# Products of constants ahead of the data, wider modulation products between the tiles, and silu rows by a broadcast load, in one layer of a diffusion backbone

## The chip, the cores and the metric

The kernel runs on one core of a Trainium2 chip. A core has five engines with queues of their own: TensorE (PE, matrix products; its weight loads are shown as PEld), VectorE (DVE), ScalarE (ACT), GpSimd (POOL) and SyncE (SP, which here only issues DMAs). They meet at semaphores. Operands lie in SBUF, products are summed in PSUM, the rest is in device memory and comes by 16 DMA engines. The metric is the device time of one execution in microseconds, lower is better.

## The reference

One layer works on 256 latent tokens and 256 context tokens of 1024 channels: a gated feed-forward layer with half a residual (both streams), a mixer of a gated delta rule and a state-space scan, and a second feed-forward layer (latent only). The change touches only what stands ahead of the first one:

```python
m  = split(silu(c)     @ w_ada + b_ada, 9)      # latent modulation, 9 x 1024
mc = split(silu(c_ctx) @ w_ada + b_ada, 9)      # context modulation
def ffn_sublayer(x, g, shift, scale, gate, w_gu, w_down):
    h = rmsnorm(x, g) * (1.0 + scale) + shift
    gt, up = split(h @ w_gu, 2)
    return x + 0.5 * gate * ((silu(gt) * up) @ w_down)
x  = ffn_sublayer(x,   norm_g[0], m[0],  m[1],  m[2],  ffn_w_gu[0], ffn_w_down[0])
xc = ffn_sublayer(ctx, norm_g[0], mc[0], mc[1], mc[2], ffn_w_gu[0], ffn_w_down[0])
```

## The kernel before

Activations are held transposed: 8 tiles (k = 0 to 7) of 128 channels on the partitions, with 512 columns, 256 of the latent stream and 256 of the context. A matrix product of full precision is made of three products of rounded operands (`mm3`, lines 213 to 215): high weight by high h, high weight by low h, low weight by high h. A weight tile is loaded (`unit`, line 192, tile `raw`), ScalarE writes its high part `whi` (198), VectorE its low part `wlo` (202). Four `raw`, three `whi` and three `wlo` buffers take turns, for the weights of all stages and for the background modulation columns alike.

`setup` (228) loads the two rows of c (`crow`), a packed constant tile (`spk`) and the four halves of x (`xl`, `xc`). silu(c) is needed twice: as columns (`cTs`, for TensorE) and as rows repeated on all 128 partitions (`cs`, for VectorE). The repeated rows are made by four products of a row of ones with the row of c (253) and four silu activations (254).

`rstd_rows` (343) squares x (ScalarE or GpSimd, by `SQS`), adds the squares, sums them over partitions by products with ones into `pss` (378), takes the reciprocal root (`rsqrt`, VectorE and then GpSimd, 337 and 341) and spreads it over the partitions by products with the identity into `psr` (383); `norm_h` copies that to `rrow` (421).

`ada_first` (274) makes scale and shift of the first norm, tile by tile. For each k there are two blocks (c = 0 shift, c = 1 scale) of a 128 x 1024 weight tile `wada`. A block named in `ADA_PE` is done on TensorE: eight products (301), each with a 128 x 128 piece as weights and two columns of `cTs` streaming, into `pada`. The other blocks are two reductions on VectorE (`ada_col`, 270), one a stream, against `cs`. Before, c = 1 is on TensorE for every k and c = 0 for k < 4. Lines 306, 310 and 311 add the bias and form scale and shift; then `norm_h` makes `ht` (430), its high part `hH` (ScalarE, 432) and its low part `hL` (435).

`ffn` (474) begins with six accumulators (three pairs of 128 output channels), for which the weights of tile k (`wgs`) come as one unit: for each k it takes h and issues 6 x 3 products of 512 columns. The remaining output tiles follow with k as the inner loop. `ada_rest` (317) is a background generator: 56 tiles `wadat` for the other modulation columns, reduced on VectorE while the feed-forward layer runs.

The kernel is written with a tile framework that sets the order of each engine's list before the run, from a priority (`cur_priority`, lower first; `wprio` for weight units), from what is ready, and from the free slots of each buffer tag. Each engine then runs its list strictly in that order. Modulation of tile k has a priority of 100000 * (k - 1) + 100 above the base, the products of tile k - 1 that of 100000 * (k - 1) + 1000: so modulation of tile k + 1 stands ahead of the products of tile k. `pada` takes turns in the PSUM tags `ch` and `sd`; `sd` has one slot, which `pss` and `psr` use too.

Of the kernel before, what the change touches and what calls it, by code (L numbers as in the profile page):

```python
# [72 lines left out]
WSP = ()  # L73
SQS = ("aaaa", "gaga")
KLO = ("dve", "dve")
# [8 lines left out]

ADA_PE = [(k, c) for k in range(8) for c in range(2) if c or k < 4]

# [51 lines left out]
class Kernel:  # L138
# [89 lines left out]
    def setup(self):  # L228
        nc, I = self.nc, self.I
        cr = [self.t4([1, D], "crow") for _ in range(2)]  # L230
        for i in range(2):
            nc.scalar.dma_start(cr[i], I["crow"][:, i])
        spk = self.const([P, 112], "spk")
# [8 lines left out]
        ones = self.ones = self.const([P, P], "ones")  # L242
        nc.vector.memset(ones, 1.0)
        self.mhalf = self.const([P, 1], "mhalf")
        nc.vector.memset(self.mhalf, -0.5)

        self.cTs = self.const([P, KD, 2], "cTs")
        nc.scalar.activation(self.cTs, cT, AF.Silu)
        self.cs = [self.kt([P, D], "cs") for _ in range(2)]
        for i in range(2):  # L250
            for j in range(2):
                pc = self.mm4(2 * i + j)
                nc.tensor.matmul(pc, ones[0:1], cr[i][:, 512 * j:512 * j + 512], start=True, stop=True)
                nc.scalar.activation(self.cs[i][:, 512 * j:512 * j + 512], pc, AF.Silu)
        self.junk = self.t4([P, D], "junk")
# [18 lines left out]
    def ada_first(self):  # L274
# [8 lines left out]
        def load():  # L283
            k = len(loads)
            if k < KD:
                loads.append([self.tp.tile([P, 2, 512], F32, tag="ring", bufs=3, name="wada").rearrange("p a b -> p (a b)")
                              if t == "ring" else getattr(self, t)([P, D], "wada") for t in WAT[k]])
                keep, self.tc.cur_priority = self.tc.cur_priority, base + 100000 * k
                for c in range(2):
                    nc.sync.dma_start(loads[k][c], self.I["wada01"][k, c])  # L290
                self.tc.cur_priority = keep
        for k in range(LDA):
            load()
        for k in range(KD):
            w = loads[k]
            self.tc.cur_priority = base + 100000 * (k - 1) + 100
            pa = self.smp([P, 2, 2], "pada", ("ch", "sd")[k % 2])
            for c in range(2):
                if (k, c) in ADA_PE:
                    for q in range(KD):  # L300
                        nc.tensor.matmul(pa[:, c], w[c][:, q * P:q * P + P], self.cTs[:, q], start=q == 0, stop=q == KD - 1)  # L301
            for c in range(2):
                a = ad[:, k, c]
                b = self.b_ada[:, 8 * c + k:8 * c + k + 1].to_broadcast([P, 2])
                if (k, c) in ADA_PE:
                    V.tensor_tensor(a, pa[:, c], b, op=ALU.add)
                    continue
# [5 lines left out]
            load()  # L313
            self.tc.cur_priority = base + 100000 * k + 1000
            yield sc[:, k], ad[:, k, 0]

# [26 lines left out]
    def rstd_rows(self, streams, name, tag="sd"):  # L343
# [6 lines left out]
        for i, s in enumerate(streams):  # L350
            a = self.t2([P, 2, NL], "sqa")
            b = self.t2([P, 2, NL], "sqb")
            if nt == 4:
                for j in range(4):
# [4 lines left out]
                    else:  # L359
                        nc.gpsimd.tensor_tensor(q, xj, xj, op=ALU.mult)  # L360
                    if j:
# [20 lines left out]
        for t in range(nt):  # L382
            nc.tensor.matmul(pr[:, t * P:t * P + P], r[:, t:t + 1].to_broadcast([P, P]), self.ident, start=True, stop=True)
        return pr

# [88 lines left out]
    def ffn(self, i, hg_, n, bg):  # L474
# [8 lines left out]
        if nf:  # L483
# [4 lines left out]
            if i == 0:  # L488
                for hH, hL, k, cols in hg_:
                    wh, wl = self.unit(I["wgs0"][k], "dve")  # L490
                    for j, a in enumerate(first):
                        sl = slice(j * P, j * P + P)
                        self.mm3(a, wh[:, sl], wl[:, sl], hH[k], hL[k], k == 0, k == KD - 1)
            else:
                hg_ = self.norm_h(2, NL)
# [1132 lines left out]
```

## Time and profile before

| | us |
|---|---|
| three runs | 1342.9, 1339.09, 5015.55 |
| median of them | 1342.9 |
| the profiled execution | 1346.67 |
| its span, first to last instruction | 1345.0 |
| its mean granted TensorE clock | 0.97 |

A profile shows one execution. For each engine it gives the time in which an instruction was under way and the idle time with what ended it; a table of windows gives these for stretches of the span, and the chain of waits follows the work that ended last back to its start. A TensorE row can overlap the next one: the ends of products are modelled, and the distance of their starts is the better measure. In the list of products an f32 product counts as two instructions.

Where the first stage (the six accumulators) lies in the profiled execution: first modulation product at 11.07 us, first product of the stage at 29.83, its last tile from 81.14 on, and the stage's end at 85.3.

### The profile page before, as it was taken

To read this page: it belongs to the slowest core of one execution; us is meant where nothing else is said; L and a number is where in the kernel's file an instruction comes from. 1 tells how busy PE (TensorE), PEld (TensorE's weight loads), DVE (VectorE), ACT (ScalarE), POOL (GpSimd) and SP (SyncE) were. 2 spreads that over 40 slices of the span, in tenths; PEclk is the share of its full clock that TensorE was granted. 3 is DMA by queue.
4 is the path that set the end of the run, shared out by engine and by line. 5 is a ranking of instruction groups with operands and counts; after the bars stand their busy time and mean duration, and the time that the engine had idled before them with its cause. 6 is when DMAs were issued, how large, how long until landed. Compare 5 with 4: busy or idle time off the path is not lost.

```text
span 1345.0 us, 21303 instructions
## 1 busy us (share of the span) xinstructions
PE 1290.2 (96%) x8224; PEld 1108.4 (82%) x8224; DVE 955.1 (71%) x1666; ACT 501.3 (37%) x935; POOL 155.1 (12%) x123
## 2 busy tenths in 40 slices
PE   8999999999999987999899999998899899999997
PEld 6878888888889876889888888854468899999997
DVE  4599387646667976888677788988774466866565
ACT  3222222212236652445423465422223345634433
POOL 1000000000010131000123111333411001000000
PEclk9899999999999988999898999998899899999998
DMA  9256357736632389656542255453446555555552
GB/s 363 92 179 221 118 188 242 233 109 235 214 106 102 110 178 242 193 184 192 153 128 80 93 174 164 150 183 125 162 144 226 174 191 190 192 189 185 179 185 79
DMA packets 133018, 230.27 MB, mean 171 GB/s; under 512 B 46706, under 2 KB 78898, under 8 KB 132788
## 3 DMA queue, kind: packets, MB, share of 16 engines
q1 hardware_dynamic: 106240, 211.43, 49.2%
q10 hardware_dynamic: 26676, 17.47, 4.2%
q8 instruction: 65, 1.06, 0.3%
q14 instruction: 37, 0.30, 0.1%
HBM read 207.79 MB, written 21.07 MB: 170 GB/s over the span
## 4 chain that ended last, share of the span: by engine, by line
PE 64%; issue 15%; DVE 13%; DMA 5%; ACT 1%; POOL 1%; SPq 1%; DVEq 0%; POOLq 0%; ACTq 0%
PE acc L213 16%; PE acc L214 16%; PE acc L215 16%; PE acc L611 3%; PE pada L301 2%; DVE Es L1437 2%; DVE cv L630 2%; DVE Es L1426 1%; PE pn L1227 1%; PE pP L1218 1%; PE pS L1253 1%; DMA Es<-asd 1%; PE pTx L1139 1%; PE ptm L980 1%; DVE Es L1439 1%
## 5 line engine op out<-in xcount | busy, mean ns | idle before, releaser
L198 ACT CAST whi<-raw 128x1024 fp32r<-128x1024 f32 (+1 forms) x208 | 214.4, 1033 | 448.9 <-PE acc L214 397.7
L213 PE MATMUL acc<-hH,whi 128*128 128x512 f32 (+1 forms) x976 | 346.5, 357 | 3.6 <-ACT hH L432 1.8
L214 PE MATMUL acc<-hL,whi 128*128 128x512 f32 (+1 forms) x976 | 345.7, 354 | 0.0
L215 PE MATMUL acc<-hH,wlo 128*128 128x512 f32 (+1 forms) x976 | 344.8, 354 | 0.0
L202 DVE TENSOR_TENSOR wlo<-raw,whi 128x1024 fp32r<-128x1024 f32 (+1 forms) x208 | 251.3, 1210 | 96.1 <-ACT whi L198 94.3
L213 PEld LDWEIGHTS acc<-hH,whi 128*128 128x128 f32 x976 | 186.5, 191 | 27.8 <-ACT hH L432 2.2
L215 PEld LDWEIGHTS acc<-hH,wlo 128*128 128x128 f32 x976 | 186.6, 191 | 23.9
L214 PEld LDWEIGHTS acc<-hL,whi 128*128 128x128 f32 x976 | 186.6, 191 | 22.9
L270 DVE CUSTOM_DVE_ANT_0 junk<-wadat,cs 128x1024 f32<-128x1024 f32 x80 | 97.8, 1222 | 42.4 <-DMA wadat<-in_wadaT 41.7
L214 PE MATMUL acc<-aL,whi 128*128 128x256 f32 (+1 forms) x384 | 122.9, 323 | 0.0
L215 PE MATMUL acc<-aH,wlo 128*128 128x256 f32 (+1 forms) x384 | 122.3, 323 | 0.0
L213 PE MATMUL acc<-aH,whi 128*128 128x256 f32 (+1 forms) x384 | 122.2, 323 | 0.0
L630 DVE SCALAR_TENSOR_TENSOR cv<-cbuf,cc,cv 128x512 f32<-128x512 f32 (+1 forms) x144 | 107.3, 752 | 4.6 <-ACT cv L628 2.6
L611 PE MATMUL acc<-hF,raw 128*128 128x256 f32 x416 | 97.7, 391 | 8.4 <-ACT gth L1071 7.8
L611 PEld LDWEIGHTS acc<-hF,raw 128*128 128x128 f32 x416 | 80.8, 197 | 22.7 <-ACT gth L1071 9.1
L214 PEld LDWEIGHTS acc<-aL,whi 128*128 128x128 f32 x384 | 73.0, 190 | 5.6
L215 PEld LDWEIGHTS acc<-aH,wlo 128*128 128x128 f32 x384 | 72.7, 190 | 5.7
L213 PEld LDWEIGHTS acc<-aH,whi 128*128 128x128 f32 x384 | 72.6, 190 | 5.6
L567 DVE SCALAR_TENSOR_TENSOR xl<-acc,hg,xl 128x256 f32<-128x256 f32 x64 | 30.3, 482 | 47.0 <-PE acc L215 46.5
L1049 PE MATMUL acc<-raw,hF 128*128 128x512 f32 x128 | 59.4, 606 | 0.6 <-DVE zbt L1053 0.6
L372 POOL TENSOR_TENSOR sqa<-sqa,sqb 128x256 f32<-128x256 f32 x12 | 11.5, 962 | 410.6 <-ACT sqb L370 407.7
L1049 PEld LDWEIGHTS acc<-raw,hF 128*128 128x128 f32 x128 | 24.6, 194 | 30.5 <-issue 28.4
(398 smaller groups left out, 2084.0 us busy)
## 6 DMA issues: line engine op xcount, KB each, us to landing
raw<-in_wgu SPq DMA_DIRECT2D x76, 512.0 KB, 3.5
wadat<-in_wadaT SPq DMA_DIRECT2D x56, 512.0 KB, 4.2
raw<-in_wdn SPq DMA_DIRECT2D x44, 512.0 KB, 3.4
wada<-in_wada SPq DMA_DIRECT2D x16, 512.0 KB, 8.9
raw<-in_wg SPq DMA_DIRECT2D x16, 512.0 KB, 3.7
raw<-in_wxs SPq DMA_DIRECT2D x16, 512.0 KB, 3.7
Es<-asd SPq DMA_DIRECT2D x16, 512.0 KB, 4.6
raw<-in_wzB SPq DMA_DIRECT2D x16, 512.0 KB, 3.9
```

The costliest lines, as they stand in the source:

```text
L198: nc.scalar.copy(hi, raw)
L202: engs[i % len(engs)].tensor_tensor(lo[:, c:c + w], raw[:, c:c + w], hi[:, c:c + w].bitcast(F32), op=ALU.subtract)
L213: mm(acc, wh, xh, start=start, stop=False)
L214: mm(acc, wh, xl, start=False, stop=False)
L215: mm(acc, wl, xh, start=False, stop=stop)
L270: self.nc.vector.tensor_tensor_reduce(out=self.junk, in0=w, in1=self.cs[s], scale=1.0, scalar=0.0, op0=ALU.mult, op1=ALU.add, accum_out=out)
L301: nc.tensor.matmul(pa[:, c], w[c][:, q * P:q * P + P], self.cTs[:, q], start=q == 0, stop=q == KD - 1)
L567: nc.vector.scalar_tensor_tensor(out=xs, in0=acc[:, NL * s - g0:NL * s - g0 + NL], scalar=hg[s][:, m:m + 1], in1=xs, op0=ALU.mult, op1=ALU ...
L611: self.nc.tensor.matmul(acc, w[:, k * P:k * P + P], self.hF[:, k], start=k == 0, stop=k == KD - 1)
L630: nc.vector.scalar_tensor_tensor(out=u3, in0=buf[:, 0:R, j:j + 64], scalar=cw[:, j:j + 1], in1=u3, op0=ALU.mult, op1=ALU.add)
L1049: nc.tensor.matmul(accs[t], self.hF[:, k, sl], w[:, wsl], start=k == 0, stop=k == 7)
L1437: V.scalar_tensor_tensor(out=B[:, j], in0=cb(1), scalar=col(self.dt, 1, j), in1=B[:, j], op0=ALU.mult, op1=ALU.add)
```

## The change

At the start, 24 products of ones by ones are issued, and silu of one column of ones. The rows of c are loaded repeated on 128 partitions and turned to silu in place, at a priority between the modulation tiles 1 and 2. Modulation weights of tiles 0 and 1 get the priority of the start, and the weight units of the first stage are put between the modulation tiles. On TensorE the modulation products now stream 128 columns (the two columns repeated 64 times), and those of tile k + 1 are issued in portions behind each of the six accumulators of tile k. c = 0 is on TensorE only for k < 2. One square of the context moves from GpSimd to VectorE, and two products are issued behind those into `psr`. Results keep their values; only the repeated columns of `pada` and the product of constants are extra.

```diff
-SQS = ("aaaa", "gaga")
+SQS = ("aaaa", "gava")
+
+WARM = (24, 2)
...
-ADA_PE = [(k, c) for k in range(8) for c in range(2) if c or k < 4]
+ADA_PE = [(k, c) for k in range(8) for c in range(2) if c or k < 2]
...
-        cr = [self.t4([1, D], "crow") for _ in range(2)]
-        for i in range(2):
-            nc.scalar.dma_start(cr[i], I["crow"][:, i])
         spk = self.const([P, 112], "spk")
         nc.scalar.dma_start(spk, I["spk"])
...
         nc.vector.memset(ones, 1.0)
+
+        warm = self.smp([P, P], "warm", "mg")
+        for _ in range(WARM[0]):
+            nc.tensor.matmul(warm, ones, ones, start=True, stop=True)
+        first = self.const([P, 1], "first")
+        nc.scalar.activation(first, ones[:, 0:1], AF.Silu)
...
         self.cs = [self.kt([P, D], "cs") for _ in range(2)]
+        keep, self.tc.cur_priority = self.tc.cur_priority, self.tc.cur_priority + 150000
         for i in range(2):
-            for j in range(2):
-                pc = self.mm4(2 * i + j)
-                nc.tensor.matmul(pc, ones[0:1], cr[i][:, 512 * j:512 * j + 512], start=True, stop=True)
-                nc.scalar.activation(self.cs[i][:, 512 * j:512 * j + 512], pc, AF.Silu)
+            nc.sync.dma_start(self.cs[i], I["crow"][:, i].to_broadcast([P, D]))
+            nc.scalar.activation(self.cs[i], self.cs[i], AF.Silu)
+        self.tc.cur_priority = keep
...
-                keep, self.tc.cur_priority = self.tc.cur_priority, base + 100000 * k
+                keep, self.tc.cur_priority = self.tc.cur_priority, base + (100000 * k if k > 1 else 10)
...
+        def pada(k):
+
+            pa = self.smp([P, 2, P // 2, 2], "pada", ("ch", "sd")[k % 2])
+            mm = lambda c, q: nc.tensor.matmul(pa[:, c], loads[k][c][:, q * P:q * P + P],
+                                               self.cTs[:, q:q + 1].to_broadcast([P, P // 2, 2]), start=q == 0, stop=q == KD - 1)
+            return pa, [lambda c=c, q=q: mm(c, q) for c in range(2) if (k, c) in ADA_PE for q in range(KD)]
+        self.tc.cur_priority = base
+        pa, self.pend = pada(0)
         for k in range(KD):
             w = loads[k]
-            self.tc.cur_priority = base + 100000 * (k - 1) + 100
-            pa = self.smp([P, 2, 2], "pada", ("ch", "sd")[k % 2])
-            for c in range(2):
-                if (k, c) in ADA_PE:
-                    for q in range(KD):
-                        nc.tensor.matmul(pa[:, c], w[c][:, q * P:q * P + P], self.cTs[:, q], start=q == 0, stop=q == KD - 1)
+            while self.pend:
+                self.pend.pop(0)()
+            self.tc.cur_priority = base + 100000 * k + 100
...
-                    V.tensor_tensor(a, pa[:, c], b, op=ALU.add)
+                    V.tensor_tensor(a, pa[:, c, 0], b, op=ALU.add)
...
             self.tc.cur_priority = base + 100000 * k + 1000
+            self.wprio = base + 100000 * k + 50
+            if k < KD - 1:
+                pa, self.pend = pada(k + 1)
             yield sc[:, k], ad[:, k, 0]
...
-                        nc.gpsimd.tensor_tensor(q, xj, xj, op=ALU.mult)
+                        (nc.vector if SQS[i][j] == "v" else nc.gpsimd).tensor_tensor(q, xj, xj, op=ALU.mult)
...
+        if nt == 4:
+            warm = self.smp([P, P], "warm", "mg")
+            for _ in range(WARM[1]):
+                nc.tensor.matmul(warm, r[:, 0:1].to_broadcast([P, P]), self.ident, start=True, stop=True)
         return pr
...
                         self.mm3(a, wh[:, sl], wl[:, sl], hH[k], hL[k], k == 0, k == KD - 1)
+
+                        for _ in range(-(-len(self.pend) // (nf - j))):
+                            self.pend.pop(0)()
+                self.wprio = 2000000
```

## The prediction

> **What bounds the kernel now.** I read the page first, then a table by stage of the first 85 us, then the chain of waits and the timeline there, because every edit but one constant acts in that stretch.
>
> ```profile
> span 1345.0 us, 21303 instructions
> PE 1290.2 (96%) x8224; PEld 1108.4 (82%) x8224; DVE 955.1 (71%) x1666; ACT 501.3 (37%) x935; POOL 155.1 (12%) x123
> ```
>
> TensorE is busy for 96% of the span, so the kernel ends when PE has done its list; time is won only where PE waits or runs slowly. The rows below have, after the window, its length, then the busy time of PE, PEld, DVE, ACT, POOL, the granted clock, DMA share and GB/s.
>
> ```profile
> 23.00:30.00 7.00, 7.00 (x33) 7.00 (x34) 5.19 (x10) 3.19 (x5) 0.00 (x0) 1.00 1.04 408
> 30.00:37.00 7.00, 7.00 (x20) 5.47 (x20) 6.85 (x16) 1.00 (x3) 0.00 (x0) 1.00 0.52 204
> 37.00:41.30 4.30, 4.30 (x33) 4.30 (x32) 1.06 (x4) 0.74 (x1) 0.00 (x0) 0.78 0.36 126
> 41.30:47.60 6.30, 6.30 (x19) 4.96 (x20) 4.51 (x12) 0.91 (x2) 0.00 (x0) 0.61 0.42 144
> ...
> 81.20:85.30 4.10, 4.10 (x18) 3.41 (x19) 3.56 (x8) 1.20 (x2) 0.00 (x0) 1.00 0.53 183
> ```
>
> PE looks full, but the same work takes different times. The chain shows it (start, length, what):
>
> ```profile
> 11.07 6.96 PE pada L301 x32
> 18.03 0.87 PE pss L378 x4
> 19.16 1.02 POOL rstd L341
> 20.23 2.09 PE psr L383 x8
> 22.34 0.59 ACT rrow L421
> 22.98 6.99 PE pada L301 x32
> 29.97 1.06 PE acc L213 x2
> 31.03 0.43 PE acc L214
> ...
> 36.60 0.23 PE acc L214
> ...
> 55.67 1.68 PE pada L301 x16
> 57.35 0.35 PE acc L213
> ...
> 61.60 1.68 PE pada L301 x16
> ```
>
> One product of 512 columns takes 0.43 us before 36 us and 0.23 us after it; 32 modulation products of 2 columns take 6.96 us (217 ns each) and later 16 take 1.68 (105 ns each). So PE runs at half speed until it has streamed dense products for some 6 us (29.97 to 36.0). The windows' clock column says 1.00 there, which the durations contradict; it registers a cold clock only later: 0.78 over 4.3 us is 1.9 us at half, so the clock fell 2.4 us into the 2-column products at 36.9, and 0.61 over 6.3 us is another 4.9 us at half. In the warm stretch one tile costs PE 5.93 us (55.67 to 61.60): 1.68 of modulation and 4.25 of 18 products. First-stage PE work ends at 85.3 us.
>
> **The change, part by part.**
>
> *24 products of constants.* They need only the ones.
>
> ```profile
> 0.90 0.17 DVE L243 MEMSET ones<- 128x128 f32 x1 [0.90 <-PEq L1618]
> 2.35 7.16 PE L253 MATMUL acc<-crow,ones 1*128 1x512 f32 x8 [2.35 <-DMA crow<-in_crow]
> ```
>
> Each f32 product is two instructions (4 row products are 8 here), so 48, from about 1.1 us. Cold at 0.217 us, warm at 0.106: after 6 us cold 28 are done, the other 20 take 2.1, end at 9.2 us. The first modulation waits for its weights until 11.07 either way, so these cost nothing; the cover is that load. The row products that go (7.16 us on PE, one partition tall) streamed 512 columns without a gap and did not wake the clock, as the 217 ns products behind them show; I take it that 128 partitions do, as the dense products did. I expect PE warm at 11.07: the gap from 9.2 is 1.9 us, under the 2.4 us after which the clock fell.
>
> [...]
>
> *128 columns instead of 2.* A modulation product costs the weight load, 105 ns, at 2 columns. For 128 columns the nearest rows are the row products of the last norm and small groups of transposes.
>
> ```profile
> 1149.85 0.61 PE L383 MATMUL psr<-ident,rstd 128*128 128x128 f32 x4
> 1150.22 0.36 PE L213 MATMUL acc<-xH,whi 128*128 128x258 f32 x1
> L980 PE MATMUL ptm<-ident,cv 128*128 128x128 f32 x96 | 14.8, 274 | 0.0
> ```
>
> Four start to the next within 0.37 us (93 ns each); in groups with a tail it is 14.8/96 = 154. I take 106: a long run has no tails. The ends over 160 instructions are -2 and +8 us. What it should buy is that the clock stays up through modulation.
>
> *Two more blocks to VectorE (k = 2, 3; c = 0).* 32 instructions leave PE (12 blocks x 16 = 192 before, 160 now), and four reductions join DVE.
>
> ```profile
> L301 PE MATMUL pada<-cTs,wada x192: 165/251/374, 11.1 to 74.9; 128*128 128x2 f32 x192
> L270 DVE CUSTOM_DVE_ANT_0 junk<-wada,cs 128x1024 f32<-128x1024 f32 x8 | 9.8, 1221 | 2.4 <-DMA wada<-in_wada 2.2
> 51.47 0.23 DVE L306 TENSOR_TENSOR ada<-pada,spk 128x2 f32<-128x2 f32 x2 [1.83 <-PE pada L301]
> 51.93 0.48 DVE L430 SCALAR_TENSOR_TENSOR ht<-xl,sc,rrow 128x256 f32<-128x256 f32 x1
> 52.45 0.91 ACT L432 ACTIVATE hH<-ht,ada 128x256 fp32r<-128x256 f32 x2 [3.79 <-DVE ht L430]
> 56.39 0.96 DVE L202 TENSOR_TENSOR wlo<-raw,whi 128x768 fp32r<-128x768 f32 x1 [2.51 <-ACT whi L198]
> 58.84 0.89 DVE L435 SCALAR_TENSOR_TENSOR hL<-ht,ada,hH 128x256 fp32r<-128x256 f32 x2 [0.18 <-ACT hH L432]
> ```
>
> From 56.39 to 59.7 DVE spends 3.3 us on one tile; two reductions and an add make 2.65, so 5.95 for each of k = 2 to 7 against PE's 5.93. DVE becomes an equal partner: from the first low part (about 15.5 us) 2 x 3.4 + 6 x 5.95 = 42.5, to 58 at the earliest, and with its waits about 61 for the last tile's h.
>
> *Silu rows by broadcast.* Four products and four activations become two 512 KB loads on SP and two activations of 128x1024.
>
> ```profile
> Es<-asd SPq DMA_DIRECT2D x16, 512.0 KB, 4.6
> 23.47 0.83 ACT L198 CAST whi<-raw 128x768 fp32r<-128x768 f32 x1 [0.54 <-DMA raw<-in_wgs]
> ```
>
> This kernel's other 512 KB broadcast lands in 4.6 us, so it is an ordinary load. It adds 1.05 MB, 2.6 us at the 408 GB/s of 23 to 30 us. With the new priorities the order is the two first modulation tiles, two small weight tiles, the rows, the third tile: weights k = 0 land at 11.07 + 1.44 MB/0.408 = 14.6 us instead of 23.4, the rows at about 18.1 and the third tile at 20.7, when its reduction first needs them. SP issues two DMAs more; those queued behind (tiles 2 to 7 and their weights) move 2.6 us later, 3.5 us per tile against 5.9 that PE needs. Cost nothing; the cover is that lead. If ACT meets the rows' silu ahead of rrow it waits: 0 to 3 us, I take 0.
>
> *The square on VectorE and the early silu.* A POOL square gives way to one of DVE, under 1 us earlier, hidden under the first modulation; the table load moves into the wait for x. 0. Two products behind psr (4 instructions, 0.4 us) fall into the wait for ht: 0.
>
> *Modulation amid products.* Tile k+1's modulation is issued in portions behind each of tile k's six accumulators, the last one behind the last product. The chain from modulation to both halves of hH is 1.9 us (51.47 to 53.36). Before, a whole tile of products covered it; now PE would wait at the head of the next tile, everything of PE queued behind. But other ready products can be put into that wait: before, the squares' second four products stand behind 32 modulation products that are written after them, so the order follows readiness too. The following tile's modulation (1.68) fills 1.9 but for some 0.2 to 0.3, and then the tile after has no wait. I take 1 us in all; ends 0 and 7 x 1.9 = 13.3.
>
> **Sum, in the profiled execution.** First modulation 11.07 + 32 x 0.106 = 14.5 (before 18.03). Sums of squares 0.5: 15.0. To psr 1.35 as before: 16.4; psr 8 x 0.106 = 0.85 and rrow 0.59: 17.85. ht and hH 1.5: the first product at 19.4 instead of 29.97; meanwhile 14 of the second modulation's 32 are done. From there 8 x 4.25 + 18 x 0.106 + 6 x 1.68 = 46.0: 65.4. With 1 us of waits and 0.6 for DVE, 67.0. Gain 85.3 - 67 = 18.3 us.
>
> What comes back later:
>
> ```profile
> L270 DVE CUSTOM_DVE_ANT_0 junk<-wadat,cs x8: 1218/1225/1227, 66.4 to 84.1; 128x1024 f32<-128x1024 f32 x8
> 75.02 1.22 DVE L202 TENSOR_TENSOR wlo<-raw,whi 128x1024 fp32r<-128x1024 f32 x1
> 85.30:107.00 21.70, 21.70 (x97) 17.96 (x97) 21.46 (x40) 5.70 (x7) 0.00 (x0) 1.00 0.59 194
> ```
>
> Before, DVE had done 8 of the 80 background columns by 85.3 and the first low part of the next weights 9.1 us before PE used it (76.2 to 85.3). After, DVE has no idle time to do the 8 (10.2 us), and afterwards it was already 99% busy (21.46 of 21.70). The loss lies between 0 (slack covers) and 6; I take 2.3. PE stays full later, so the rest goes through: 16 us. The profiled execution took 1346.7 (span 1345.0 and 1.7 around it): 1330.7. It stands 3.8 over the median 1342.9, so I predict **1327**.
>
> **Rivals.**
> 1. *Waits unfilled*: the order holds the written sequence; each tile waits 1.9. For it: nothing but readiness fills. Against: the order before. 13.3 instead of 1 and 0.6: 79 us, and DVE has time for the 8 columns: gain 6, 1337.
> 2. *Clock stays cold until the products*: constants done too early, or the dip to rrow cools it. For: row products of 7.16 us woke nothing. Then the first product starts about 24.4 and its tile, cold for 6 us, ends near 34; seven warm tiles and their modulation 39.8, 1 of wait: 75; gain 10, less 2.3: 1335. [...]
> 3. *Slower*: DVE meets a tile's two reductions in the chain, so that each head waits 1.9 + 2.65 = 4.55. Seven make 31.9: 65.4 + 31.9 = 97.3, 12 us slower: 1355. It decides from 19.9/7 = 2.8 us a tile. For: DVE's 5.95 of 5.93. Against: the reductions' data land 3.5 us apart and can be done ahead.
> 4. *All of it*: no waits, no debt, 93 ns products: 64 us, gain 21 to 23: 1321.
>
> **How the numbers follow.** Forecast 0.52 (own range 1322 to 1332), rival 1 0.17, rival 2 0.13, rival 3 0.08, rival 4 0.10. Low end 1315, below rival 4 by a few us of change in later order; high end 1342, which leaves out most of rival 3. Two per cent, about what a measurement of this kernel can tell from no change, is 27 us: PE work of 17 + 34 + 2 us from 11.07 on ends no earlier than 64, so faster needs luck later: 0.05. Slower by 27 us needs rival 3 at 6.7 us a tile: 0.03. Within: 0.92.
>
> **What would show it.** Right: modulation products at 105 ns from 11 us on, 512-column products at 0.23 from the first; first product near 19.4, last of the stage near 67; DVE full from 20 to 61; wlo of the next weights close to PE's use. Wrong: 0.43 products after 20 us (rival 2); PE idle 1.9 us at each tile head behind hH (rival 1), or behind the reductions (rival 3); a product of the second stage waiting for wlo by over 2.3 us in all.

## The result and the profile after

The changed kernel takes 1330.28 us (median of 17 runs, 1323.68 to 1342.70) against 1343.87 for the kernel before on the same chips (median of 17). The ratio is 0.9917 with a 95% interval of [0.9896, 0.9938]: a gain of 0.6 to 1.0 per cent, real, and within the 2% that counts as no change. The profiled execution took 1335.1 us with a span of 1333.4, 11.6 less than the 1345.0 before.

The first and third line of the page of the changed kernel:

```profile
span 1333.4 us, 21355 instructions
PE 1273.7 (96%) x8236; PEld 1099.2 (82%) x8236; DVE 956.1 (72%) x1675; ACT 500.1 (38%) x933; POOL 157.3 (12%) x122
```

TensorE is still busy for 96% of the span and has lost 16.5 us of busy time, while DVE, ACT and POOL are where they were. So the question is again what PE does in the first stage. Its timeline there (start, length, line, what, count; in brackets the idle time before and what ended it):

```profile
1.12 7.61 PE L246 MATMUL warm<-ones 128*128 128x128 f32 x48 [1.12 <-DVE mhalf L250]
9.86 0.61 PE L392 MATMUL pss<-ones,sqa 128*128 128x1 f32 x4 [1.14 <-DVE sqa L379]
10.67 5.44 PE L303 MATMUL pada<-cTs,wada 128*128 128x128 f32 x32 [0.20 <-DMA wada<-in_wada]
15.95 0.50 PE L392 MATMUL pss<-ones,sqa 128*128 128x1 f32 x4
18.45 1.65 PE L397 MATMUL psr<-ident,rstd 128*128 128x128 f32 x8 [2.00 <-POOL rstd L355]
19.90 1.06 PE L401 MATMUL warm<-ident,rstd 128*128 128x128 f32 x4
20.78 4.58 PE L303 MATMUL pada<-cTs,wada 128*128 128x128 f32 x32
25.12 1.64 PE L215 MATMUL acc<-hH,whi 128*128 128x512 f32 x6
```

The constants end before the modulation's weights land. The first modulation takes 5.44 us where 32 products at full speed take some 3.6 (the second modulation of e4 below), the second 4.58. The products of 512 columns begin 4.71 us earlier than before and are at full speed from the first one on: six in 1.64, where before two took 1.20:

```profile
29.83 1.20 PE L213 MATMUL acc<-hH,whi 128*128 128x512 f32 x2
```

The windows (length, busy time of PE, PEld, DVE, ACT, POOL, granted clock, DMA share, GB/s) tell when the clock was low:

```profile
12.00:13.00 1.00, 1.00 (x8) 1.00 (x7) 0.96 (x2) 0.00 (x0) 0.00 (x0) 0.57 1.02 418
15.00:15.95 0.95, 0.95 (x8) 0.95 (x7) 0.00 (x0) 0.57 (x1) 0.00 (x0) 0.71 1.07 419
18.45:20.00 1.55, 1.54 (x9) 1.55 (x10) 0.00 (x0) 0.00 (x0) 0.10 (x1) 0.66 1.03 412
22.00:23.00 1.00, 1.00 (x10) 1.00 (x9) 0.91 (x2) 1.00 (x2) 0.00 (x0) 0.81 1.02 409
63.00:64.00 1.00, 1.00 (x5) 0.78 (x4) 1.00 (x4) 0.00 (x0) 0.00 (x0) 0.83 0.00 0
```

A window that lies wholly between a fall and a rise has 0.50 granted (13 to 14 us), and the modulation's products there start 213 ns apart, where they are 112 apart ahead of the fall. A mean of 0.57 is then 0.86 us at half speed, so the clock fell at 12.14. In the same way it rose at 15.55, fell at 18.95, rose at 22.38, and rose again at 63.34. The steps are 3.41, 3.40, 3.43 and 40.96 = 12 x 3.41, and in the trace's record of the clock all changes of this execution, from 5.30 us to 1326.26, are whole multiples of 3.41 us apart, in the mixer as in the first stage. A step of this grid is what the expectations below call the clock window. Where the grid lies differs between the two profiles of this kernel: in the second one (e12 below) the first fall is at 11.16.

Later in the stage there is one wait. PE's timeline, then DVE's:

```profile
58.53 1.78 PE L215 MATMUL acc<-hH,whi 128*128 128x512 f32 x6 [1.81 <-ACT hH L450]
60.79 0.79 PE L216 MATMUL acc<-hL,whi 128*128 128x512 f32 x1 [0.48 <-DVE hL L453]
```

```profile
53.18 1.22 DVE L275 CUSTOM_DVE_ANT_0 junk<-wadat,cs 128x1024 f32<-128x1024 f32 x1 [0.51 <-DMA wadat<-in_wadaT]
55.70 1.22 DVE L275 CUSTOM_DVE_ANT_0 junk<-wadat,cs 128x1024 f32<-128x1024 f32 x1
57.06 0.48 DVE L448 SCALAR_TENSOR_TENSOR ht<-xl,sc,rrow 128x256 f32<-128x256 f32 x1
```

At 58.53 the sixth of the eight tiles begins: a tile has 18 products, and 90 of them lie ahead. (The expectations below call it the seventh.) Ahead of its ht DVE did background columns (wadat), PE stood still for 1.81 and 0.48 us, and behind this the clock was down too (0.83 granted from 63 to 64 is the end of it): the six products up to 63.3 start 0.43 us apart instead of 0.23. So this place costs 1.81 + 0.48 + 6 x 0.2 = 3.5 us. The other tile heads have no wait of note. The eight tiles have 144 products; the last one starts at 72.74, and the next stage begins with the one behind it, which is the first to wait for new weights:

```profile
72.74 0.39 PE L217 MATMUL acc<-hH,wlo 128*128 128x512 f32 x1
72.97 0.39 PE L215 MATMUL acc<-hH,whi 128*128 128x512 f32 x1
```

In the kernel before the product behind the 144th starts at 85.35, so 12.4 us are won at the stage's end. (The expectations, 71.6 to 71.8, leave out the last six products.) The stage in one row:

```profile
25.10:72.97 47.87, 45.58 (x243) 38.75 (x242) 42.33 (x95) 14.01 (x24) 0.20 (x1) 0.96 0.58 212
```

Two landmarks follow the gain through the rest: the first weight load of hF (first feed-forward done) and the first of xH. I call the stretch between them the mixer. Before, then after, the group of hF (duration min/median/max in ns, first and last start) and the mixer's window:

```profile
L611 PEld LDWEIGHTS acc<-hF,raw x416: 186/190/337, 476.3 to 1034.8; 128*128 128x128 f32 x139
476.30:1142.40 666.10, 628.12 (x4344) 518.86 (x4343) 496.62 (x872) 267.16 (x548) 132.86 (x94) 0.95 0.55 167
```

```profile
L633 PEld LDWEIGHTS acc<-hF,raw x416: 186/190/337, 463.1 to 1021.5; 128*128 128x128 f32 x139
463.10:1131.10 668.00, 625.57 (x4344) 518.30 (x4343) 494.24 (x872) 267.36 (x548) 135.66 (x94) 0.95 0.55 166
```

At the stage's end 12.4 us are won, at hF 13.2, and 1.9 are lost in the mixer, which the diff does not touch: PE is busy there for 2.5 us less, but waits 42.4 us instead of 38.0 (length less PE busy). After it the changed kernel needs 0.3 us less.

### The profile page after: what moved, and what is told of

The parts are those of the page before. It is cut to its first block, busy times and chain, and to the rows that moved or that the text cites. A ratio compares the mean times of both kernels' runs of the same rounds, so it can differ in the third digit from the quotient of the medians.

```text
span 1333.4 us, 21355 instructions
## 1 busy us (share of the span) xinstructions
PE 1273.7 (96%) x8236; PEld 1099.2 (82%) x8236; DVE 956.1 (72%) x1675; ACT 500.1 (38%) x933; POOL 157.3 (12%) x122
## 4 chain that ended last, share of the span: by engine, by line
PE 65%; issue 15%; DVE 8%; DMA 7%; ACT 2%; SPq 1%; POOL 1%; POOLq 0%; DVEq 0%; ACTq 0%
PE acc L216 16%; PE acc L215 16%; PE acc L217 16%; PE acc L633 3%; PE acc L1071 2%; PE pada L303 1%; DVE cv L652 1%; DMA RB<-gsd 1%; DMA zAsc<-zth 1%; PE pyd L1464 1%; PE pSs L1392 1%; PE pP L1240 1%; PE pn L1249 1%; DVE Es L1448 1%; PE ptm L1002 1%
## 5 line engine op out<-in xcount | busy, mean ns | idle before, releaser
L215 PE MATMUL acc<-hH,whi 128*128 128x512 f32 (+1 forms) x976 | 340.3, 354 | 2.8 <-ACT hH L450 1.8
L386 POOL TENSOR_TENSOR sqa<-sqa,sqb 128x256 f32<-128x256 f32 x12 | 12.4, 1035 | 417.0 <-ACT sqb L384 414.1
```

Of the source, the lines that this page charges most:

```text
L215: mm(acc, wh, xh, start=start, stop=False)
```

## The experiments

The questions: which edit wins what in the first stage; what the clock there depends on; whether the sixth tile's wait is DVE's background work; and why a stretch that nobody edited changes its length. On the last one, two theories: the order of its instructions is drawn anew by the scheduler when anything ahead of it changes; or the order is the same and the execution scatters.

All kernels, with the ratio to the kernel before (on the same chips in the same round; its medians there are 1342.2 to 1343.9), the median, the lowest and highest run and their number, the start of the first 512-column product, what is won at hF, and the length of the mixer. The list column gives one letter to kernels whose compiled TensorE instructions between the landmarks (3068 entries, buffer numbers left out) are the same in the same order.

```
kernel                  ratio [95%]               median   runs (number)        first   hF won  mixer  list
before                                            1343.87                       29.83     0.0   666.1   O
the change              0.9917 [0.9896, 0.9938]   1330.28  1323.7..1342.7 (17)  25.12    13.2   668.0   P
e1_no_constants         0.9878 [0.9851, 0.9904]   1324.67  1323.3..1326.4 (4)   24.24    17.0   663.3   S
e2_two_columns          1.0066 [1.0030, 1.0102]   1349.89  1347.7..1356.4 (6)   28.52     3.3   672.9   Q
e3_bridged              0.9877 [0.9843, 0.9911]   1324.26  1321.6..1328.4 (4)   25.89    16.9   665.2   S
e4_bg_later             0.9943 [0.9920, 0.9965]   1334.06  1330.8..1339.0 (10)  21.75    18.1   671.4   Q
e5_before_wide          1.0030 [1.0005, 1.0054]   1346.48  1337.3..1351.4 (10)  28.01     9.2   673.2   T
e6_ahead                0.9859 [0.9833, 0.9884]   1321.34  1320.9..1325.5 (4)   25.08    16.7   658.3   R
e7_four_blocks          0.9916 [0.9888, 0.9945]   1328.86  1324.1..1335.1 (6)   25.52    12.8   660.9   U
e8_rows_by_products     0.9852 [0.9830, 0.9873]   1321.27  1320.3..1322.3 (4)   25.64    17.6   657.9   R
e9_ahead_late           0.9953 [0.9927, 0.9979]   1337.64  1329.9..1342.7 (10)  21.78    19.5   668.8   Q
e10_rows_bg             0.9868 [0.9834, 0.9902]   1326.41  1322.2..1330.8 (6)   26.11    16.6   662.4   R
e11_square_on_pool      0.9923 [0.9892, 0.9954]   1332.23  1327.0..1344.6 (10)  24.30    10.0   674.3   P
e12_change_again        one run                   1335.41                       24.00    10.9   666.3   P
```

**No constants.** Both numbers go to 0, which also drops the two products behind psr.

```diff
-WARM = (24, 2)
+WARM = (0, 0)
```

> The changed kernel without its products of constants (24 at the start, two behind psr). In the profile of the changed kernel the first modulation ran 5.44 us (10.67 to 16.11), the clock falling at 12.1 us and back at 15.5. Theory A (the constants hold the clock up for the first modulation, as the prediction had it): without them the first modulation runs wholly cold, 32 x 0.217 = 7.0 us, the second too, the first product of 512 columns starts 3 to 5 us later than 25.1, and the whole takes 3 to 5 us more than the changed kernel (ratio to before 0.994 to 0.996). Theory B (the constants end a whole clock window too early and buy little): the first modulation gets warm after 3.4 to 6.8 us of its own streaming, first product at 25 to 26.5, whole time within 1.5 us of the changed kernel (ratio 0.991 to 0.993).

Measured (PE's timeline):

```profile
11.19 5.28 PE L303 MATMUL pada<-cTs,wada 128*128 128x128 f32 x26 [1.12 <-DMA wada<-in_wada]
24.24 1.64 PE L215 MATMUL acc<-hH,whi 128*128 128x512 f32 x6
```

The first modulation (26 products in 5.28 us, the other six in 0.91) wakes the clock by itself (the second one takes 3.84 us for its 32, as in e4 below), and the first 512-column product starts no later than with constants. In this pair of profiles the constants buy nothing. No tile head waits here for over 0.2 us: with the sixth tile's 3.5 us gone and the first product 0.9 earlier, 4.4 were to come, and 3.8 are there at hF. The median is 5.6 us under that of the change, which neither theory had; the mixer, with another list, is 4.7 shorter.

**Two columns again**, the rest of the change kept.

```diff
-pa = self.smp([P, 2, P // 2, 2], "pada", ...)
+pa = self.smp([P, 2, 1, 2], "pada", ...)
-self.cTs[:, q:q + 1].to_broadcast([P, P // 2, 2])
+self.cTs[:, q:q + 1].to_broadcast([P, 1, 2])
```

> The changed kernel with modulation products of 2 columns as before, everything else kept. Theory A (128 columns are what counts as activity): both first modulations run at 217 ns a product (7.0 us each), the clock is still low when the products of 512 columns start, at about 29, and those run at 0.43 us for 3.4 to 7 us: the six-accumulator stage ends 6 to 10 us later than the changed kernel's 71.8, the time is 6 to 10 us more (ratio to before 0.996 to 0.999). Theory B (width is irrelevant, order and constants do it): modulation products as fast as in the changed kernel, stage end within 1.5 us of 71.8, ratio 0.991 to 0.993.

Measured:

```profile
22.10 6.56 PE L303 MATMUL pada<-cTs,wada 128*128 128x2 f32 x30 [0.68 <-ACT rrow L439]
28.52 2.91 PE L215 MATMUL acc<-hH,whi 128*128 128x512 f32 x6
68.72 2.93 PE L215 MATMUL acc<-hH,whi 128*128 128x512 f32 x6 [1.92 <-ACT hH L450]
```

The 512-column products start cold again (six in 2.91 us, not 1.64), the second modulation runs at some 218 ns a product (30 in 6.56 us), and of the 13.2 us at hF 3.3 are left. The width is the edit that wins the stage. In this execution products of two columns neither kept the clock up nor woke it: by the trace's record of the clock it fell at 13.24, 2.4 us into the first modulation (10.86 on), and came back at 33.73, 5.2 us into the 512-column products. By the medians e2 is 19.6 us slower than the change, more than the 6 to 10 expected; in the profiles 9.9 are lost at hF and 4.8 in the mixer, where its list is another.

**The kernel before with 128 columns alone** (the same three places edited in it) is the other half of this:

> The kernel before with one edit: its modulation products stream 128 columns instead of 2. Theory A (the width is what wakes and holds the clock, the rest of the change adds little): the first modulation wakes the clock by itself within 3.4 to 6.8 us, the second runs at about 110 ns a product, all products of 512 columns at 0.23 us; the stage ends at 72 to 76 instead of 85.3 and the time falls by 9 to 13 us (ratio 0.990 to 0.993), nearly all that the whole change gains. Theory B (the width pays only with the earlier weights and the order of the change): the stage ends at 79 or later, ratio 0.995 or more.

Measured: 9.2 us are won at hF, the largest single share, yet 7.1 are lost in the mixer (673.2, with another list), and the kernel as a whole is not faster (1.0030 [1.0005, 1.0054]). Whoever looks at the total alone would call this edit useless.

**The clock bridged to the products of the norm:** 36 constants, and eight more products on the squares behind pss.

```diff
-WARM = (24, 2)
+WARM = (36, 2, 4)
...
         if nt == 4:
+            warm = self.smp([P, P], "warm", "mg")
+            for _ in range(WARM[2]):
+                for q, t in parts[-2:]:
+                    nc.tensor.matmul(warm, q, self.ones, start=True, stop=True)
         r = self.const([P, nt], name)
```

> The changed kernel with 36 constants instead of 24, so that they reach to the first modulation, and eight more products of 128 columns behind the squares' sums, which fill the wait for the reciprocal root. Theory A (the free window of 3.41 us fell on the idle stretches 8.7 to 10.7 and 16.4 to 18.4, and this cost the start): the clock stays up from about 5 us on, first modulation 3.4 to 3.6 us instead of 5.44, psr 0.9 instead of 1.65, second modulation 3.4 instead of 4.58, first product of 512 columns at 20.5 to 22 instead of 25.1, and the stage ends 3 to 4 us earlier than 71.8. Theory B (VectorE is the bound of the stage, 95% busy from 25 to 60): the start is earlier, but the wait at the seventh tile grows by the same amount, the stage ends within 1 us of 71.8 and the time does not change.

Measured, PE's timeline and ACT's:

```profile
11.23 2.70 PE L303 MATMUL pada<-cTs,wada 128*128 128x128 f32 x22
17.12 1.05 PE L402 MATMUL psr<-ident,rstd 128*128 128x128 f32 x8
20.67 5.47 PE L303 MATMUL pada<-cTs,wada 128*128 128x128 f32 x32 [2.04 <-ACT rrow L444]
25.89 1.63 PE L215 MATMUL acc<-hH,whi 128*128 128x512 f32 x6
```

```profile
19.09 1.06 ACT L258 ACTIVATE cs<-cs 128x1024 f32<-128x1024 f32 x1 [0.46 <-DMA cs<-in_crow]
20.05 0.57 ACT L444 COPY rrow<-psr 128x512 f32<-128x512 f32 x1
```

The clock stayed up: psr starts 1.33 us earlier and takes 1.05. Then ACT was at the silu of a row that landed at 18.6 to 19.1, which stands ahead of rrow in its list; PE stood 2.04 us, the clock fell, and the second modulation took 5.47. What was won ahead is lost behind: a wait that the prediction put at 0 to 3 us and took as 0 showed up once psr was early enough to meet it.

**Background columns one tile later.**

```diff
-if bg is not None and m0 + m > 2:
+if bg is not None and m0 + m > 3:
```

> The changed kernel with the background columns begun one output tile later, so that none of them lies in VectorE's list ahead of the h of the last two tiles. Theory A (in the changed kernel three background reductions of 1.15 us stand in that list between 53.2 and 60.3 and make most of the wait of PE from 56.7 to 60.8, which then costs a cold clock from 59.9 to 63.3): the wait at the seventh tile shrinks from 4.1 us (with 6 products in it) to 1.5 to 2, no cold products there, the stage ends at 67 to 69 instead of 71.8, and the whole is 2 to 5 us faster than the changed kernel (ratio to before 0.988 to 0.990). Theory B (the columns must be done anyway and VectorE is full afterwards): the stage ends earlier, but the time is given back before the first-layer down projection: products waiting for wlo, ratio 0.991 to 0.993.

Measured:

```profile
10.82 3.81 PE L303 MATMUL pada<-cTs,wada 128*128 128x128 f32 x32 [0.53 <-DMA wada<-in_wada]
16.32 1.16 PE L397 MATMUL psr<-ident,rstd 128*128 128x128 f32 x8 [1.34 <-POOL rstd L355]
18.15 3.84 PE L303 MATMUL pada<-cTs,wada 128*128 128x128 f32 x32 [0.23 <-ACT rrow L439]
21.75 1.63 PE L215 MATMUL acc<-hH,whi 128*128 128x512 f32 x6
53.73 1.65 PE L215 MATMUL acc<-hH,whi 128*128 128x512 f32 x6 [0.39 <-ACT hH L450]
```

The sixth tile's wait falls from 1.81 to 0.39 us. DVE's compiled list is that of the change up to the first background column, so the wait was DVE's background work. The start is 3.4 us better with the same instructions in the same order: this execution kept its clock (1.00 granted from 10.8 to 14.5 us, from 18.1 to 21.7 and from 25.1 to 71.6). At the stage's end (66.25) 19.1 us are won, where the prediction had 18.3, and 18.1 at hF. The mixer, with another list, gives 3.4 more back than that of the change, and in all the edit wins nothing (0.9943 against 0.9917, with intervals that overlap).

**Portions of modulation ahead of the products**, instead of amid them (while self.pend: self.pend.pop(0)() stands ahead of the loop over the accumulators).

> The changed kernel with the modulation of tile k+1 written ahead of the products of tile k, not in portions behind its accumulators. Theory A (each engine's list follows readiness, so the written portions hardly matter): the lists differ in few places, the stage ends within 1 us of 71.8 but for the clock window's phase, which alone can move it by 3.4 us; ratio 0.988 to 0.993. Theory B (the portions cover the chain to h): without them PE waits 1.9 us at several tile heads, stage end 76 or later, ratio 0.995 or more.

Measured: the first product starts at 25.08, as in the change (25.12), and no tile head waits, the sixth neither: its ht stands at 52.55 in DVE's list, ahead of the first background column at 53.34. At hF 3.5 us more are won (16.7 against 13.2), just the price of that place. The mixer's list is another too, and 658.3 us long; in all 0.9859. So portions amid the products are no better here than portions ahead of them. That the place is gone is not owed to this edit alone: e1, with its portions amid, has no wait there either, since the background work there too was drawn in another order.

**Four blocks instead of two taken back by PE.**

```diff
-... if c or k < 2]
+... if c or k < 4]
```

> The changed kernel with c = 0 on TensorE for k < 4 as before. PE gets 32 instructions more (3.6 us at 0.113), VectorE four reductions less (5.1 us). Theory A (VectorE is the partner bound, its list makes the wait at the seventh tile): that wait of 4.1 us and the cold clock behind it (1.6 us) go, so the stage ends 1 to 3 us earlier than 71.8 in spite of PE's extra work. Theory B (PE is the bound): the stage ends 3 to 4 us later, at 75, ratio 0.994.

Measured: 12.8 won at hF against 13.2, 0.9916 against 0.9917. The stage ends at 72.79, which neither theory had (72.97 in the change). The sixth tile's wait is gone here too (3.5 us), and 32 more products on PE at 0.112 (e4's second modulation, 18.15 to 21.75 for 32) make 3.6: the two cancel.

**Rows by products as before**, the rest of the change kept (the lines that the diff takes away put back, the broadcast loads and their two activations removed).

> The changed kernel with the silu rows made as before, by four products of a row of ones and four activations. Theory A (the broadcast load costs 2.6 us of transfer and two long activations that stand in ScalarE's list around rrow and hH): the weights of tiles 2 and later come 2.6 us earlier, the first h is ready 1 to 2 us earlier, the stage ends 1 to 3 us earlier than 71.8. Theory B (the products at the start push the constants back and keep the clock low): the first modulation runs at 217 ns, the stage ends 2 to 4 us later.

Measured: 17.6 won at hF, mixer 657.9, 0.9852. The row products push the first modulation to 13.74 and the first product to 25.64, 0.5 later than in the change; the sixth tile has no wait (3.5 us). That makes 16.2 of the 17.6. The broadcast loads, then, brought no more than half a microsecond at the start, and the kernel without them is the faster one in the end.

**One number.** e6 with the rows' priority moved on; nothing is added or removed.

```diff
-... self.tc.cur_priority + 150000
+... self.tc.cur_priority + 250000
```

> The kernel of e6 (modulation ahead of products) with one number changed: the repeated rows of c are loaded at a priority behind modulation tile 2 instead of ahead of it. The first stage changes by little (first hF product within 4 us of e6's 459.6), but TensorE's list of the mixer becomes the same, entry for entry, as that of e2 and e4. Theory A (the time of the mixer is set by the list that the framework made, and any edit ahead of it draws another list): from the first hF product to the first xH product it takes 670 to 674 us, as in e2 (672.9) and e4 (671.4), against 658.3 in e6, and the whole takes 10 to 18 us more than e6 (ratio to before 0.993 to 1.000). Theory B (the differences of the mixer are chance of the single profiled execution): that stretch is anywhere from 658 to 673, and the time within 4 us of e6, ratio 0.984 to 0.989.

Measured: the first stage is better by 2.8 us at hF, the mixer's list changes from R to Q and the mixer from 658.3 to 668.8, and the medians stand 16.3 us apart (1337.64 and 1321.34), with no overlap of the runs. The profiled execution of e9 is its fastest of ten (1329.86), so the two profiles show 8.2 of the 16.3. The waits of PE in the mixer (in total, times, longest) show part of the difference, first e6, then this kernel:

```profile
PE acc L635 <- ACT gth L1095: 8.8, 2, 8.0
```

```profile
PE acc L635 <- ACT gth L1095: 14.2, 4, 9.1
```

**Two good parts together:** rows by products and the background later.

> The changed kernel with the silu rows made by products as before (e8) and the background columns begun one output tile later (e4). TensorE's list of the mixer is the same as in e6 and e8. Theory A (the gains of the first stage add, the mixer goes by its list): first hF product at 456 to 459, 657 to 660 from there to the first xH product, time 1316 to 1321 (ratio 0.981 to 0.985). Theory B (VectorE's debt of columns is paid later): first hF product at 460 or later, ratio 0.986 or more.

Measured:

```profile
13.83 4.21 PE L306 MATMUL pada<-cTs,wada 128*128 128x128 f32 x18
26.11 1.64 PE L215 MATMUL acc<-hH,whi 128*128 128x512 f32 x6
```

The list is R again, the mixer 662.4, 2.4 us over what was expected, and 16.6 are won at hF, 1 less than in e8. e8 has no wait at the sixth tile that a later background could remove. The median, 1326.41, is over the expected 1316 to 1321, and 0.9868 does not beat e6 or e8.

**Same list, other start:** the one square goes back to POOL ("gava" to "gaga").

> The changed kernel with the context's third square back on GpSimd. TensorE's list of the mixer is that of the changed kernel. If that list sets the mixer: 666 to 670 us from the first hF product to the first xH product, as the changed kernel's 668.0. In the first stage: the sums of squares are ready 0.5 to 1 us later, hidden under the first modulation, so the stage ends within 3.4 us of 71.6, by the clock window's phase alone (theory A, the square costs nothing), or the reciprocal root starts 1 us later and so does everything (theory B); ratio 0.989 to 0.994.

Measured: 674.3, 6.3 over that of the change with the same list, in an execution of 1344.58 us that is the slowest of its ten (median 1332.23). The expectation missed.

**The change once more**, nothing edited.

> The changed kernel itself, profiled once more. The list is the same, so by theory A the mixer takes 666 to 670 us again. What may differ is the phase of the clock window in the first 25 us: the first product of 512 columns anywhere from 21.5 (clock up throughout) to 25.5, and the first stage's end from 68 to 72.

Measured:

```profile
10.79 5.44 PE L303 MATMUL pada<-cTs,wada 128*128 128x128 f32 x32
24.00 1.63 PE L215 MATMUL acc<-hH,whi 128*128 128x512 f32 x6
57.42 1.66 PE L215 MATMUL acc<-hH,whi 128*128 128x512 f32 x6 [1.81 <-ACT hH L450]
...
11.00:12.00 1.00, 1.00 (x7) 1.00 (x7) 0.97 (x2) 0.00 (x0) 0.00 (x0) 0.58 1.06 434
58.00:59.00 1.00, 1.00 (x5) 0.56 (x3) 1.00 (x2) 0.17 (x1) 0.00 (x0) 0.97 0.57 229
65.00:66.00 1.00, 1.00 (x4) 0.82 (x3) 0.10 (x1) 0.86 (x1) 0.00 (x0) 0.62 0.00 0
465.40:1131.70 666.30, 625.67 (x4345) 516.00 (x4344) 495.48 (x872) 267.56 (x548) 132.42 (x94) 0.96 0.54 167
```

The mixer is within 1.7 us of the first profile. The clock fell at 11.16 (0.58 is 0.84 us at half), not at 12.14, and the first product came 1.1 us earlier. But behind the same wait at the sixth tile the clock was down from 58.94 to 65.76, two periods of 3.41 us instead of the one in the first profile, and 3.41 more at half speed are worth 1.7, an estimate. The stage ends 0.6 later (73.53, or 72.2 as the expectation counts), and another 1.8 are lost before hF, where the clock is at half for 3.4 us that the first profile does not have (0.57 granted from 407 to 411). So even one wait has no fixed price: it was followed by one period at half in one execution and by two in the other. e11 has the same wait (1.81 and 0.58), with the clock down over as long.

**What follows for the scheduler's order.** In the first stage the sixth tile's wait is there in the change, e11 and e12. It is absent in e1, e3, e6, e7, e8 and e10, six edits with little in common; e4 and e9 have 0.39 and 0.75 us, e2 waits 1.92 at the seventh tile and e5 1.99 at the eighth, where the kernel before has 1.76 (at 81.14). In the mixer, kernels with one list lie at 658 to 662 (R), 663 to 665 (S), 669 to 673 (Q) and 666 to 674 (P). So the mixer shifts by some 10 us with the list, which an edit far ahead redraws, and e9 against e6 shows that one changed number is enough; the execution adds up to 8 us within a list, and does so most in P, whose runs spread over 19 us (17 runs of the change) where those of e8 spread over 2 (4 runs).

Two parts of these differences can be read from the traces: how long PE waits in the mixer (length less PE busy), and how long its clock is at half there (from the trace's record of the clock, whose mean the windows show).

```
kernel                  list  mixer  PE waits  clock at half
before                  O     666.1  38.0      61.4
the change              P     668.0  42.4      64.9
e12_change_again        P     666.3  40.6      58.0
e11_square_on_pool      P     674.3  41.8      78.5
e6_ahead                R     658.3  37.9      47.8
e9_ahead_late           Q     668.8  43.5      54.6
```

A stretch at half costs up to half its length, an estimate that takes PE as busy throughout. Within P, e11 has 13.6 us more at half than the change, worth up to 6.8, with the waits alike, and its mixer is 6.3 longer: there the execution's part is the clock. From e6 to e9 PE waits 5.6 us more, and 6.8 more at half are worth 3.4; that makes 9.0 of the 10.5. From before to the change PE waits 4.4 more and 3.5 more at half are worth 1.7, but the mixer is only 1.9 longer, so the parts do not simply add. That the list is the cause of each single difference is not shown, since no run gave the changed kernel the list of before; for the 1.9 us that the change lost it stays open.

## Why the prediction came out

The forecast was 1327 us, and 1330.28 was measured, inside the range and inside the forecast's own range. Its gain of 16 us against a profiled execution became 11.6 (13.6 between the medians of 17 runs each), and some steps of the sum were off by more than that difference.

- *Constants cost nothing*: right. The modulation started at 10.67, when its weights were there.
- *"I expect PE warm at 11.07: the gap from 9.2 is 1.9 us, under the 2.4 us after which the clock fell"*: wrong, and this is the largest error. The clock fell at 12.14 in the modulation, rose, fell at 18.95, rose. The prediction took its waking time (6 us) and its falling time (2.4 us) from one pass each, as if they were counted from the start of the work. The steps of 3.41 us show a grid instead. The idle time ahead of the modulation does not tell the two outcomes apart: 1.34 us in the change, where the clock fell, and 1.30 in e9, where it stayed (1.00 granted from 10 to 25 us). The last step of the grid ahead of the fall, from 8.73 (12.14 less 3.41) to 12.14, held 1.47 us of modulation and 0.61 of pss. In e9, whose clock rose at 5.77, the step from 9.18 to 12.60 held 1.74 and 0.61. How much work in a step keeps the clock is not shown by these two. So rival 2 (0.13) happened in part, and not in every execution: here the clock fell in the first modulation and again behind the wait for psr, only the first time in e12 (1.00 granted from 15 to 25 us), and not at all in e9.
- *"To psr 1.35 as before"*: it took 2.00, by a meeting that the late modulation made. DVE's timeline of the change and POOL's, and the same two of e4:

```profile
16.57 0.96 DVE L204 TENSOR_TENSOR wlo<-raw,whi 128x768 fp32r<-128x768 f32 x1
16.73 1.67 POOL L355 TENSOR_TENSOR rstd<-rstd,mhalf 128x4 f32<-128x4 f32 x1 [7.21 <-DVE rstd L351]
```

```profile
16.40 0.96 DVE L204 TENSOR_TENSOR wlo<-raw,whi 128x768 fp32r<-128x768 f32 x1 [1.23 <-ACT whi L200]
15.25 1.01 POOL L355 TENSOR_TENSOR rstd<-rstd,mhalf 128x4 f32<-128x4 f32 x1 [5.90 <-DVE rstd L351]
```

  wlo stands behind the cast of its weights and starts at about the same time in both. In e4 the root is through by then, in the change it runs beside wlo and takes 0.66 longer. The other profiles bear it out: the root takes 1.67 in all nine in which it overlaps a wlo and 1.01 or 1.02 in all five in which it does not. The first product's 3.37 us between the two kernels are the first modulation (1.63), the root (0.66), psr (0.49) and the second modulation (0.74), less 0.15 elsewhere.
- *First product at 19.4 with 14 of the second modulation's 32 done*: the scheduler put all 32 first, so 19.4 + 18 x 0.106 = 21.3 is the number to compare. e4 and e9, whose clock stayed up, have 21.75 and 21.78; the change has 25.12. With its clock up, the sum was right to 0.5 us.
- *"I take 1 us in all"* for waits at tile heads: 3.5 measured, all at one tile, the fallen clock included. The sum gave a wait its idle time alone; that products behind it can run at half speed was left out. Rival 1 had all heads wait; one did. The cause was of rival 3's kind, DVE late, but through background columns instead of the tile's own two reductions.
- *18.3 us at the stage's end*: 12.4 measured, 5.9 less. The clock took 3.8 (25.12 less 21.3) and the sixth tile 3.5, of which 1.6 had been allowed for waits; that makes 5.7 of the 5.9.
- *"I take 2.3"* as DVE's debt: none shows at hF, where 0.8 us more are won than at the stage's end. DVE had idle time after all: it was busy 42.33 of the 47.87 us quoted above, and did 7 of the 8 background columns there that it had done before. The 0.8 are not DVE's: the kernel before has its clock at half for 3.4 us in between (0.57 granted from 418 to 422), worth 1.7, and the changed kernel has it up all the way. Without that some 0.9 us would have come back, an estimate from these two rows.
- *"PE stays full later, so the rest goes through"*: 1.9 us did not, and the experiments show that this step could have brought or cost 8 us (657.9 in e8, 674.3 in e11, against 666.1 before).
- *The balance*: 5.9 us too few at the stage's end, 3.1 more than forecast from there to hF, 1.9 lost in the mixer and 0.3 won behind it make 11.6 instead of 16. The mechanism (a warm clock and an earlier start) was right; that errors of this size left the time so near to the forecast is luck in part.
- *The width's purpose*: right. e2 takes it away and loses 9.9 of the 13.2 us at hF.
- *Silu rows by broadcast at nothing*: e3 met the wait that was named and put at zero; e8, without the broadcast, is faster.

The best kernels measured are e8 and e6 (0.9852 and 0.9859), each with one part of the change undone; by their intervals they are not clear of e10, e3 and e1.

## What to carry to other kernels

Measure an edit at landmarks along the kernel and not by the total alone: where a scheduler draws one order for everything, an edit of the first 20 us can cost or bring more in an untouched stage than in its own. Check in more than one profile what a short warm-up buys when a wait follows it: here it kept the clock through the first modulation in two of seven, and the kernel without it was no slower (0.9878 against 0.9917). And keep background work off the engine that has the next tile's inputs to make, at the tiles where that engine has no lead.

## What the hardware showed unexpectedly

- *What the constants were worth went with the clock's phase.* The constants' own duration tells the phase: in the change some 19 of the 48 start 213 ns apart, until the clock's rise at 5.30 us, and the others 112, so a later rise makes them longer (7.83 us in e9, whose clock rose at 5.77). Of the seven profiles with these constants, no row products and 128 columns, the two whose constants took longest (8.39 in e4, 7.83 in e9) kept the clock through the first modulation (3.81 both) and began the 512-column products at 21.75 and 21.78; the five with 7.14 to 7.61 (the change, e6, e7, e11, e12) paid 5.44 and began at 24.00 to 25.52. The phase was not set by any experiment, so this is an observation on seven executions.
- *A root on POOL beside DVE.* 128x4 took 1.67 us beside DVE's wlo (nine profiles) and 1.01 or 1.02 without it (five). In the change the root is 0.66 us longer than in e4, and wlo, already under way, covers the first 0.80 us of it (16.73 to 17.53). What the two share is not shown.
